# Regrouping the attention half of a transformer block, and three smaller moves: halves on GpSimd, gate tiles on SyncE's queue, block outputs in two pieces

## The chip, the cores and the metric

One Trainium2 chip, one core of it. A core has TensorE (PE: matmuls, with the weight load shown apart as PEld), VectorE (DVE), ScalarE (ACT), GpSimd (POOL) and SyncE (SP), which here only issues DMAs. ACT and POOL issue DMAs too; in the rows ACTq and SPq are the DMA issues of these engines. The metric is the device time of one execution in microseconds (us), median over runs.

## The reference

One layer on x of 1024 tokens by 1024 features, batch 1, all float32:

```
h  = rms_norm(x) ; y = h @ w_in              # q (8 heads of 64), k, v (2 heads), p (512)
a  = sliding-window attention(q, k, v)       # 64-token chunks, own and two before, q/k norm, bias, sinks
b  = pool_mixer(p)                           # trailing means over 2, 4, 8, 16 tokens, small matmuls
x  = x + concat(a, b) @ w_out
h2 = rms_norm(x)                             # "second norm"
q  = h2 @ wq ; top 16 of 128 keys, twice, for 8 heads ; top 16 of the 256 sums -> experts, gates
x  = x + sum over the 128 chosen experts of  gate * gelu(u[e] . h2) * v[e]
```

There are 128 x 128 = 16384 experts; u and v have one row of 1024 each per expert.

## The kernel before, in words

The 1024 tokens are 8 tiles of 128. Two ways of evaluating the experts stand side by side. Tiles 0, 6 and 7 are *gathered*: for each of 128 slots, GpSimd fetches one u row per token (L169), DVE takes the dot product (L190), and later the same with v rows (L197). Tiles 1 to 5 are *dense*: all experts in 128 blocks of 128, with matmuls. For a block, `load` (L227) fetches 512 KB of u into a `ur` buffer (there are three), `split` makes `uh` on ACT (L239) and the remainder `ul` on GpSimd (L244), and `u_mm` (L277) does 48 matmuls with 320 columns into two PSUM tiles, against `hh`/`hl`, the two halves of the transposed second norm of the dense tiles, which `halves` makes (L253 to L259). After gelu comes the product with the block's gates (L968), and then the v matmuls (L989).

The program has a front and a back. The front:

- `first(tiles)`: norm, projection by w_in, transposes. It is called for the sets in `FIRST`.
- `second(tiles)`: attention, pooling, the product with w_out (its weights streamed once per call, 16 DMAs of 256 KB, each split into `woh` on ACT, L357, and `wol` on DVE or GpSimd, L358, as `LOS2` says), second norm, and transposes to `h2Td` in DRAM (L668 to L670). It is called once for each entry of `GROUPS`; the tiles of one entry go through attention interleaved. `AT` says beside which group each later `first` set runs.
- `zero`: keys and top 16 for tile 0, so that its gathers can start early.
- `scores`: for the other seven tiles, 16 rounds of h2 @ wq and key scores (L782, L791), each followed on DVE by two top-8 searches per tile (`top16`, L674 to L679).
- for each tile `topk`, and for dense tiles `gates`: DVE builds one-hot tiles (L813, L820), PE multiplies them (L827), ACT evicts into `stage` (L829), and each of 20 full stage tiles of 2 MB goes out to `gd` (L833).
- `ahead`: 68 of the 128 u blocks are run in the front, as filler of the lowest priority; gelu results `wr` (L296) go to DRAM in `ad` (L297). `AHEAD0` of them are recorded beside the last group, before `scores`. The `ur` buffers are handed out in the order in which the code asks for them, and the halves of tiles 6 and 7, which `scores` needs, ask behind these blocks.

The back runs the other 60 u blocks, reads `gd` (L931) and `ad` (L953) back, and does all v matmuls; gathers run beside them.

A scheduler at build time orders the instructions of each engine; on the chip each engine runs its own list in that order, and a DMA that an engine issues waits for its inputs in the same list.

Of the kernel before, what the change touches and what calls it, by code (L numbers as in the profile page):

```python
# [8 lines left out]
F32 = mybir.dt.float32  # L9
# [5 lines left out]
AF = mybir.ActivationFunctionType  # L15
OP = mybir.AluOpType
AX = mybir.AxisListType

T, D, P = 1024, 1024, 128
# [8 lines left out]
LOW = -3.0e38  # L28


GROUPS = ((0,), (1, 2), (3, 4), (5, 6), (7,))
GSCALE = 32768.0
EARLY = 0.2
EARLY2 = 0.4
# [10 lines left out]
XB = 2  # L45
WPO = 2
WRB = 2
AHEAD0 = 8
HITP = 0
ULP = 4  # L50
VLP = 2
# [4 lines left out]
YQ = 3  # L56
WR0 = 4
SPLIT0 = 1
AT = (-1, 0, 2, 3)
GB0 = 2  # L60
WF = 3
QT = 3
# [6 lines left out]
WP = 3  # L69
XT = 1  # L70
LOS = (1, 1, 2, 2)
LOS2 = (1, 1, 1, 2, 1)
GAP = 0
AHP = 10000
VBUFS = 4
# [15 lines left out]
DT = ND * P  # L91
NH = DT // 2
# [3 lines left out]
TCH = 32  # L96
# [31 lines left out]
def body(tc, ctx, a):  # L128
    nc = tc.nc
# [4 lines left out]
    V, S, E, Q = nc.vector, nc.scalar, nc.tensor, nc.gpsimd  # L134
# [11 lines left out]
    gd = DR.tile([KEYS // CHUNK, P, NTC, CHUNK, TCH], F32, name="gd")  # L146
# [70 lines left out]
    U = {}  # L217
# [4 lines left out]
    ad = DR.tile([KEYS, P, DT], F32, name="ad")  # L222

    def load(b, h=None):
        if h is None:
            t = U["u"].tile([P, D], F32, name="ur", bufs=UR)
            nc.sync.dma_start(t, a["uT"][b].rearrange("p c e -> p (c e)"))  # L227
        else:
            t = U["v"].tile([P, 512], F32, name="vr", bufs=VR)
            nc.sync.dma_start(t, a["v"][b * KEYS:(b + 1) * KEYS, h * 512:(h + 1) * 512])  # L230
        raw[b, h] = t

    def split(b, h=None):
        t = raw.pop((b, h))
        if h is None:
            hi, lo = (U["u"].tile([P, D], F32R, name=n, bufs=2) for n in ("uh", "ul"))
        else:
            hi, lo = (U["v"].tile([P, 512], F32R, name=n, bufs=VBUFS) for n in (f"v{h}h", f"v{h}l"))
        S.activation(hi, t, AF.Copy)  # L239
        if h is None:  # L240

            for c in range(0, D, D // ULP):
                part = slice(c, c + D // ULP)
                Q.tensor_tensor(lo[:, part], t[:, part], hi[:, part], op=OP.subtract)  # L244
        elif h:
            for c in range(0, 512, 512 // VLP):
                part = slice(c, c + 512 // VLP)
                Q.tensor_tensor(lo[:, part], t[:, part], hi[:, part], op=OP.subtract)  # L248
        else:
            V.tensor_tensor(lo, t, hi, op=OP.subtract)  # L250
        us[b, h] = (hi, lo)

    def halves(i, hi, lo):  # L253
        t = U["u"].tile([P, D], F32, name="ur", bufs=UR)
        nc.sync.dma_start(t, h2Td[i])
        t3 = t.rearrange("p (c n) -> p c n", c=DC)
        S.activation(hi, t3, AF.Copy)
        V.tensor_tensor(lo, t3, hi, op=OP.subtract)
        return hi, lo  # L259

    def open_u():
# [7 lines left out]
    def u_mm(b):  # L269
        uh, ul = (t.rearrange("p (c e) -> p c e", c=DC) for t in us.pop((b, None)))  # L270
        pa = []
        after["turn"] = not after.get("turn")
        for n in range(2):
            p = PS.tile([P, 512], F32, name="pu", bufs=2) if b in soon or after["turn"] else ps()
            for k, (l, r) in enumerate(((uh, U["hh"]), (uh, U["hl"]), (ul, U["hh"]))):
                for d in range(DC):
                    E.matmul(p[:, :NH], l[:, d, :], r[:, d, n * NH:(n + 1) * NH],  # L277
                             start=(k == 0 and d == 0), stop=(k == 2 and d == DC - 1))
            pa.append(p)
        return pa  # L280

    def ahead():
        if AHEAD:
            with tc.high_priority(offset=-AHP):
                load(after[None])
                split(after[None])
        for b in soon:
            with tc.high_priority(offset=-AHP):
                if after[b] is not None:
                    load(after[b])  # L290
                pa = u_mm(b)
                if after[b] is not None:
                    split(after[b])
                t = U["u"].tile([P, DT], F32, name="wr", bufs=WRB)
                for n in range(2):
                    S.activation(t[:, n * NH:(n + 1) * NH], pa[n][:, :NH], AF.Gelu)  # L296
                nc.scalar.dma_start(ad[b], t)  # L297
            yield

    with ExitStack() as c1:  # L300
# [8 lines left out]
def front(tc, ctx, a, env):  # L309
    nc = tc.nc  # L310
    C, PS, DR, EX, ps, flow = (env[k] for k in ("C", "PS", "DR", "EX", "ps", "flow"))
    x1d, h2d, h2Td, gd = (env[k] for k in ("x1d", "h2d", "h2Td", "gd"))
    V, S, E, Q = nc.vector, nc.scalar, nc.tensor, nc.gpsimd
# [314 lines left out]
    def second(tiles):  # L628
        Y = {i: carry.pop(("first", i)) for i in tiles}
        wo = Stream(W, [a["w_out"][k] for k in range(8)], "wo", LOS2[GROUPS.index(tiles)], WPO, WRO, 1)  # L630
        if PAIR:
# [169 lines left out]
    def gates(i):  # L801
        j = DENSE.index(i)
        ekT, gT = carry["G", i]
        for q in range(P // TCH):
            sg = M.tile([P, KEYS, TCH], F32, name="stage", bufs=2)
            for r in range(TCH // TG):
                t0 = q * TCH + r * TG

                pairs = lambda x: x.rearrange("p (q w) -> p q w", w=2)[:, :, None, :].to_broadcast([P, TG // 2, P, 2])
                ob = []  # L810
                for s in range(2):
                    o = M.tile([P, TG // 2, P, 2], F16, name=f"ob{s}", bufs=OB)
                    V.tensor_tensor(o, pairs(ekT[:, s, t0:t0 + TG]),  # L813
                                    late["iote"][:, None, :, :].to_broadcast([P, TG // 2, P, 2]), op=OP.is_equal)
                    ob.append(o)
                    yield
                og = []
                for s in range(2):
                    o = M.tile([P, TG // 2, P, 2], F16, name=f"og{s}", bufs=OB)
                    V.tensor_tensor(o, ob[1], pairs(gT[:, s, t0:t0 + TG]), op=OP.mult)  # L820
                    og.append(o)
                    yield
                for h in range(TG // 4):
                    p = ps()
                    for t in range(4):
                        for s in range(2):
                            E.matmul(p[:, t * KEYS:(t + 1) * KEYS], ob[0][:, h * 2 + t // 2, :, t % 2], og[s][:, h * 2 + t // 2, :, t % 2],  # L827
                                     start=(s == 0), stop=(s == 1))
                    S.activation(sg[:, :, r * TG + h * 4:r * TG + h * 4 + 4], p.rearrange("p (t e) -> p e t", t=4),  # L829
                                 AF.Copy, scale=1.0 / GSCALE)  # L830
                    if h % 2:
                        yield
            nc.scalar.dma_start(gd[:, :, j * (P // TCH) + q].rearrange("c p e t -> p c (e t)"),  # L833
                              sg.rearrange("p (c e) t -> p c (e t)", e=CHUNK))
            yield

# [4 lines left out]
    def merge(parts, rate):  # L841
        parts = [[g, n, 0] for g, n in parts]
        total = max(n for _, n, _ in parts)
        for s in range(total):
            for part in parts:
                while part[2] * total < (s + 1) * part[1]:
                    part[2] += 1
                    next(part[0], None)
            flow(rate)
        for part in parts:  # L850
            for _ in part[0]:
                pass
# [4 lines left out]
    def lift(gen, by):  # L857
        while True:
            with tc.high_priority(offset=by):
                if next(gen, "end") == "end":  # L860
                    return
            yield
    merge([A1(FIRST[0])], 0)
    early1.close()
    W1 = early1.enter_context(tc.tile_pool(name="early1", bufs=2, reuse_waits="tile"))
    firsts = lambda k: [A1(f) for f, at in zip(FIRST, AT) if at == k]
    merge([A2(GROUPS[0])] + firsts(0), 0)
    X.open("tile0")
    M.tile = X.tile

    def zero():
        t = X.tile([P, DC, P], F32, name="h0T")
        nc.sync.dma_start(t, h2Td[0].rearrange("p (c t) -> p c t", c=DC))
        yield from scores((0,), [(t, None)], False)
        yield from topk(0)

    merge([A2(GROUPS[1]), (lift(zero(), HPZ), ZN)] + firsts(1), 0)
    X.close()
    open_g()
    for k in range(2, len(GROUPS) - 1):  # L880
        merge([A2(GROUPS[k])] + firsts(k), EARLY)
    early1.close()
    hh, hl = env["open_u"]()
    ahead = env["ahead"]()
    merge([A2(GROUPS[-1]), (islice(ahead, AHEAD0), AHEAD0)], EARLY)
    early.close()
# [11 lines left out]
    for i in ORDER:  # L898
# [3 lines left out]
        n = parts[0][1]  # L902
# [164 lines left out]
```

## Time and profile before

| | us |
|---|---|
| median of 3 runs (lowest, highest) | 2647.17 (2643.72, 2656.37) |
| profiled execution: time, span | 2642.85, 2641.1 |
| PE / DVE / POOL / ACT busy over the span | 2441.8 / 2244.3 / 1643.6 / 924.1 |

The span falls into stages, cut at events on PE: attention up to the first score matmul at 517.2; the score rounds up to 745.0; top-k and gates up to the last gate matmul at 1291.1; from there to the first v matmul at 1341.5; the back up to 2611.3; and a rest of gathers. Shares of busy time are means over stages with different limits, so they are read per stage. The profiled execution lies 4.3 us under the median of the runs.

### The profile page before, as it was taken

To read this page: it belongs to the slowest core of one execution; us is meant where nothing else is said; L and a number is where in the kernel's file an instruction comes from. 1 tells how busy PE (TensorE), PEld (TensorE's weight loads), DVE (VectorE), ACT (ScalarE), POOL (GpSimd) and SP (SyncE) were. 2 spreads that over 40 slices of the span, in tenths; PEclk is the share of its full clock that TensorE was granted. 3 is DMA by queue.
4 is the path that set the end of the run, shared out by engine and by line. 5 is a ranking of instruction groups with operands and counts; after the bars stand their busy time and mean duration, and the time that the engine had idled before them with its cause. 6 is when DMAs were issued, how large, how long until landed. Compare 5 with 4: busy or idle time off the path is not lost.

```text
span 2641.1 us, 41309 instructions
## 1 busy us (share of the span) xinstructions
PE 2441.8 (92%) x14627; PEld 2183.2 (83%) x14627; DVE 2244.3 (85%) x4236; ACT 924.1 (35%) x1701; POOL 1643.6 (62%) x1636
## 2 busy tenths in 40 slices
PE   7889776999998997989799999999999999999995
PEld 6678555999998887889798888888888888888884
DVE  4768776499999998999678888898898988889898
ACT  5646454322223444444342222322323222222221
POOL 1101765664566766666666767766777767667675
PEclk9989887999999998998899999999999999999998
DMA  7655779977677687777889999999999999999998
GB/s 238 224 172 174 263 244 314 340 241 246 213 261 256 202 270 255 218 230 252 299 286 353 356 332 348 342 329 347 340 348 336 346 348 346 326 354 335 335 332 313
DMA packets 323375, 770.22 MB, mean 292 GB/s; under 512 B 26944, under 2 KB 124128, under 8 KB 319072
## 3 DMA queue, kind: packets, MB, share of 16 engines
q0 software_dynamic: 110592, 402.70, 42.3%
q1 hardware_dynamic: 115072, 287.55, 31.9%
q10 hardware_dynamic: 97504, 77.34, 9.0%
q8 instruction: 114, 1.87, 0.3%
q14 instruction: 93, 0.76, 0.1%
HBM read 687.53 MB, written 79.95 MB: 291 GB/s over the span
## 4 chain that ended last, share of the span: by engine, by line
PE 47%; DVE 1%; issue 1%; DMA 1%; ACTq 0%; POOL 0%; ACT 0%; POOLq 0%; DVEq 0%
PE pt L989 16%; PE ps L989 16%; PE pu L277 8%; PE pt L277 4%; PE ps L277 4%; DVE vec L197 1%; DMA row<-v,idx 1%; ACTq L297 0%; POOL row L169 0%; DVE wl L977 0%; DVE wb L968 0%; DVE acc L994 0%; ACT wh L975 0%; ACT uh L239 0%; ACT row L200 0%
## 5 line engine op out<-in xcount | busy, mean ns | idle before, releaser
L244 POOL TENSOR_TENSOR ul<-ur,uh 128x256 fp32r<-128x256 f32 x512 | 462.3, 934 | 113.8 <-ACT uh L239 70.4
L169 POOL DMA_INDIRECT row<-v,idx x301 | 347.3, 1154 | 230.7 <-DVE vec L197 137.9
L169 POOL DMA_INDIRECT row<-u,idx x306 | 313.4, 1024 | 243.6 <-DVE row L190 118.8
L190 DVE SCALAR_TENSOR_TENSOR row<-row,vec 128x1024 f32<-128x1024 f32 x306 | 368.0, 1212 | 75.6 <-DMA row<-u,idx 72.2
L197 DVE SCALAR_TENSOR_TENSOR vec<-row,act,vec 128x1024 f32<-128x1024 f32 x301 | 385.6, 1281 | 25.4 <-DMA row<-v,idx 22.1
L277 PE MATMUL pu<-hh,uh 128*128 128x320 f32 x1568 | 283.3, 318 | 40.6 <-ACT wr L296 40.2
L277 PE MATMUL pu<-hh,ul 128*128 128x320 f32 x1568 | 281.7, 316 | 18.9 <-POOL ul L244 18.5
L277 PEld LDWEIGHTS pu<-hh,uh 128*128 128x128 f32 x1568 | 246.0, 193 | 54.1 <-ACT wr L296 48.9
L277 PE MATMUL pu<-hl,uh 128*128 128x320 f32 x1568 | 276.7, 314 | 0.0
L277 PEld LDWEIGHTS pu<-hh,ul 128*128 128x128 f32 x1568 | 246.0, 192 | 24.8 <-POOL ul L244 21.8
L277 PEld LDWEIGHTS pu<-hl,uh 128*128 128x128 f32 x1568 | 246.8, 192 | 2.7
L248 POOL TENSOR_TENSOR v1l<-vr,v1h 128x256 fp32r<-128x256 f32 x256 | 210.4, 848 | 11.8 <-ACT v1h L239 8.9
L239 ACT ACTIVATE uh<-ur 128x1024 fp32r<-128x1024 f32 x128 | 135.1, 1058 | 235.4 <-PE pu L277 126.3
L975 ACT ACTIVATE wh<-wb 128x640 fp32r<-128x640 f32 x128 | 91.6, 735 | 216.6 <-PE ps L989 123.0
L239 ACT ACTIVATE v0h<-vr 128x512 fp32r<-128x512 f32 x128 | 80.5, 631 | 241.2 <-DMA vr<-v 151.9
L989 PE MATMUL pt<-v0h,wh 128*128 128x512 f32 x384 | 150.6, 392 | 3.3 <-ACT wh L975 2.6
L989 PE MATMUL pt<-v0h,wl 128*128 128x512 f32 x384 | 150.6, 393 | 0.2 <-DVE wl L977 0.2
L989 PE MATMUL pt<-v0l,wh 128*128 128x512 f32 x384 | 149.7, 390 | 0.0
L989 PE MATMUL ps<-v1h,wh 128*128 128x512 f32 x384 | 149.4, 389 | 0.0
L989 PE MATMUL ps<-v1h,wl 128*128 128x512 f32 x384 | 149.4, 389 | 0.0
L989 PE MATMUL ps<-v1l,wh 128*128 128x512 f32 x384 | 149.4, 389 | 0.0
L994 DVE TENSOR_TENSOR acc<-pt,acc 128x512 f32<-128x512 f32 x155 | 106.2, 685 | 42.9 <-PE pt L989 42.5
(267 smaller groups left out, 5846.6 us busy)
## 6 DMA issues: line engine op xcount, KB each, us to landing
ur<-uT SPq DMA_DIRECT2D x128, 512.0 KB, 4.7
vr<-v SPq DMA_DIRECT2D x256, 256.0 KB, 6.1
gd<-stage ACTq DMA_DIRECT2D x20, 2048.0 KB, 12.3
g<-gd SPq DMA_DIRECT2D x32, 1280.0 KB, 8.5
ad<-wr ACTq DMA_DIRECT2D x68, 320.0 KB, 5.2
wb<-ad SPq DMA_DIRECT2D x68, 320.0 KB, 6.7
wo<-w_out SPq DMA_DIRECT2D x80, 256.0 KB, 4.2
wi<-w_in SPq DMA_DIRECT2D x32, 512.0 KB, 4.7
```

The lines of the kernel that those rows point to most:

```text
L169: Q.indirect_dma_start(out=r, out_offset=None, in_=tabs[s], in_offset=bass.IndirectOffsetOnAxis(ap=EX[i][0][:, k:k + 1], axis=0))
L190: V.scalar_tensor_tensor(r, r, 1.0, vec, op0=OP.mult, op1=OP.mult, accum_out=st["act"][:, k:k + 1])
L197: V.scalar_tensor_tensor(vec, r, st["gl"][:, k:k + 1], vec, op0=OP.mult, op1=OP.add)
L239: S.activation(hi, t, AF.Copy)
L244: Q.tensor_tensor(lo[:, part], t[:, part], hi[:, part], op=OP.subtract)
L248: Q.tensor_tensor(lo[:, part], t[:, part], hi[:, part], op=OP.subtract)
L277: E.matmul(p[:, :NH], l[:, d, :], r[:, d, n * NH:(n + 1) * NH], start=(k == 0 and d == 0), stop=(k == 2 and d == DC - 1))
L975: S.activation(wh, wr, AF.Copy)
L989: E.matmul(p, l[:, j * P:(j + 1) * P], r, start=(m == 0 and k == 0), stop=(m == CHUNK - 1 and k == 2))
L994: V.tensor_tensor(part, p, part, op=OP.add)
```

## The change

`GROUPS` has four pairs, so w_out is streamed four times; `LOS2` and `AT` follow (`first` of tiles 5, 6 now runs beside the group (2, 3) and tile 0's keys, `first` of tile 7 beside (4, 5)). `AHEAD0` goes from 8 to 12. The remainder in `halves` is taken by GpSimd. Each `wr` is two tiles of 320 columns, each sent by its own DMA. The gate tiles are sent by SyncE in place of ScalarE.

```diff
-GROUPS = ((0,), (1, 2), (3, 4), (5, 6), (7,))
+GROUPS = ((0, 1), (2, 3), (4, 5), (6, 7))
-AHEAD0 = 8
+AHEAD0 = 12
-AT = (-1, 0, 2, 3)
+AT = (-1, 0, 1, 2)
-LOS2 = (1, 1, 1, 2, 1)
+LOS2 = (1, 1, 2, 1)
@@ halves
-        V.tensor_tensor(lo, t3, hi, op=OP.subtract)
+        Q.tensor_tensor(lo, t3, hi, op=OP.subtract)
@@ ahead
-                t = U["u"].tile([P, DT], F32, name="wr", bufs=WRB)
                 for n in range(2):
-                    S.activation(t[:, n * NH:(n + 1) * NH], pa[n][:, :NH], AF.Gelu)
-                nc.scalar.dma_start(ad[b], t)
+                    t = U["u"].tile([P, NH], F32, name="wr", bufs=2 * WRB)
+                    S.activation(t, pa[n][:, :NH], AF.Gelu)
+                    nc.scalar.dma_start(ad[b, :, n * NH:(n + 1) * NH], t)
@@ gates
-            nc.scalar.dma_start(gd[:, :, j * (P // TCH) + q].rearrange("c p e t -> p c (e t)"),
+            nc.sync.dma_start(gd[:, :, j * (P // TCH) + q].rearrange("c p e t -> p c (e t)"),
```

PE's list at the first round of scores. In the names `uh`, `ul` are a u block's halves, `wqh`, `wql` those of wq, `gh`, `gl` those of the second norm of tiles 6 and 7, and `sk` the keys (L791 gives one tile's scores). Before:

```order
L782 MATMUL ps<-hh,wqh 128x320 x8
L782 MATMUL ps<-hl,wqh 128x320 x8
L782 MATMUL pt<-hh,wqh 128x320 x8
L782 MATMUL pt<-hl,wqh 128x320 x8
L782 MATMUL ps<-gh,wqh 128x256 x3
L782 MATMUL ps<-hh,wql 128x320 x8
L782 MATMUL pt<-hh,wql 128x320 x8
L782 MATMUL ps<-gh,wqh 128x256 x5
L782 MATMUL ps<-gl,wqh 128x256 x8
L782 MATMUL ps<-gh,wql 128x256 x8
L791 MATMUL pt<-sk,qT 128x128 x2
```

And now, from the last piece of the round's dense part:

```order
L277 MATMUL pu<-hl,uh 128x320 x5
L791 MATMUL pt<-sk,qT 128x128 x2
L277 MATMUL pu<-hl,uh 128x320 x3
L277 MATMUL pu<-hh,ul 128x320
L791 MATMUL pt<-sk,qT 128x128 x2
L782 MATMUL pt<-hh,wqh 128x320 x8
L782 MATMUL pt<-hl,wqh 128x320 x8
L782 MATMUL pt<-hh,wql 128x320 x8
L277 MATMUL pu<-hh,ul 128x320 x7
L277 MATMUL pu<-hh,uh 128x320 x8
L277 MATMUL pu<-hl,uh 128x320 x8
```

The round was one piece, with the `gh` matmuls of tiles 6 and 7 inside; now the `gh` part is not there: four tiles are scored, the next round's dense part goes first, and u blocks follow, 151 matmuls in a row. Counted over the whole list, 433 u matmuls stood before the round's last score and 586 do now (48 are a block); before the last L668 it was 311 and is 216.

SyncE's list in the gate stage (`ur<-uT` is the load of a u block, `gd<-stage` a gate tile). Before:

```order
L758 DMA wq<-wq 128x1024
L759 DMA sk<-skT 128x128
L181 DMA rowx<-x1d 128x1024
L227 DMA ur<-uT 128x1024 x55
L230 DMA vr<-v 128x512 x3
L931 DMA g<-gd 128x2560 x2
```

And now:

```order
L181 DMA rowx<-x1d 128x1024
L227 DMA ur<-uT 128x1024 x18
L833 DMA gd<-stage 128x32x128
L227 DMA ur<-uT 128x1024 x2
L833 DMA gd<-stage 128x32x128 x2
L227 DMA ur<-uT 128x1024 x2
L833 DMA gd<-stage 128x32x128
L227 DMA ur<-uT 128x1024 x4
L833 DMA gd<-stage 128x32x128
L227 DMA ur<-uT 128x1024
```

The 20 gate tiles stand between loads of u blocks, mostly one to five loads apart.

ScalarE's list at the last gate tile. Before:

```order
L829 ACTIVATE stage<-ps 128x128x4
L296 ACTIVATE wr<-pu 128x320 x2
L833 DMA gd<-stage 128x32x128
L297 DMA ad<-wr 128x640
L239 ACTIVATE uh<-ur 128x1024
L296 ACTIVATE wr<-pu 128x320
L297 DMA ad<-wr 128x640
```

And now:

```order
L297 DMA ad<-wr 128x320
L829 ACTIVATE stage<-pt 128x128x4
L297 DMA ad<-wr 128x320
L829 ACTIVATE stage<-ps 128x128x4
L961 ACTIVATE pu<-pu 128x320
L239 ACTIVATE uh<-ur 128x1024
L296 ACTIVATE wr<-pu 128x320
L297 DMA ad<-wr 128x320
```

No gate tile is issued between ACT's own work any more, and the first block of the back (L961) comes sooner: PE's list has 216 u matmuls between the last gate matmul and the first v matmul, and had 269.

## Rows read from the trace of the kernel before

**Rows 1.** Windows of the stages: length, busy us (xinstructions), clock, DMA share, GB/s.

```profile
core 0: us, PE busy (x) PEld busy (x) DVE busy (x) ACT busy (x) POOL busy (x), PEclk, DMA share, GB/s
0.00:517.20 517.20, 427.41 (x2404) 346.16 (x2405) 351.40 (x761) 270.26 (x624) 199.19 (x185) 0.92 0.73 243
517.20:745.00 227.80, 216.62 (x1573) 213.93 (x1572) 207.29 (x912) 59.60 (x110) 124.23 (x110) 0.99 0.72 242
745.00:1291.10 546.10, 486.50 (x3856) 468.44 (x3855) 522.28 (x1003) 229.38 (x378) 373.09 (x307) 0.95 0.75 244
1291.10:1341.50 50.40, 41.69 (x274) 41.16 (x272) 20.73 (x23) 14.61 (x25) 27.85 (x34) 0.93 0.91 326
1341.50:2611.30 1269.80, 1266.30 (x6516) 1111.17 (x6515) 1119.82 (x1521) 349.26 (x564) 907.92 (x988) 1.00 0.94 339
```

**Rows 2.** Chain that ended last, one u block: start us, us, what.

```profile
1327.54 7.04 PE pu L277 x48
```

**Rows 3.** Timeline of PE, first scores: start us, us, engine, line, op.

```profile
533.17 0.61 PE L791 MATMUL ps<-sk,qT 128*128 128x128 f32 x4
```

**Rows 4.** Windows of the attention stage, columns as in rows 1.

```profile
64.00:145.00 81.00, 62.68 (x343) 49.27 (x344) 60.91 (x129) 60.71 (x160) 14.00 (x12) 0.89 0.67 214
...
340.00:428.00 88.00, 62.63 (x310) 43.82 (x308) 63.72 (x103) 47.30 (x117) 55.70 (x47) 0.87 0.76 251
428.00:500.00 72.00, 65.26 (x381) 58.58 (x380) 43.29 (x67) 27.32 (x43) 44.51 (x52) 0.88 0.94 334
sum 436.00, PE 359.27 PEld 289.71 DVE 316.06 ACT 230.89 POOL 181.69; mean PE 71.85 PEld 57.94 DVE 63.21 ACT 46.18 POOL 36.34
```

**Rows 5.** Timeline of PE, two of its idles there, in brackets with the releaser.

```profile
76.39 1.94 PE L533 MATMUL ps<-ident,prob 128*128 128x128 f32 x8 [5.71 <-ACT xh L586]
...
423.82 2.93 PE L668 MATMUL pt<-ident,x 128*128 128x128 f32 x12 [8.61 <-DVE x L660]
```

**Rows 6.** Lines L258 and L773: ns min/median/max, first and last start.

```profile
L258 DVE TENSOR_TENSOR gl<-ur,gh x2: 1219/1220/1221, 509.4 to 519.4; 128x1024 fp32r<-128x1024 f32 x2
...
L773 POOL TENSOR_TENSOR wql<-wq,wqh x16: 2376/2406/2432, 521.4 to 714.1; 128x1024 fp32r<-128x1024 f32 x16
```

**Rows 7.** Waits of DVE, 745 to 1291.1: us in total, times, longest.

```profile
DVE vec L197 <- DMA rowx<-v,idx: 6.8, 5, 3.2
DVE gate L726 <- PE ps L743: 6.1, 1, 6.1
```

**Rows 8.** Waits of PE in the same stretch.

```profile
PE pu L277 <- ACT wr L296: 31.5, 22, 5.3
```

**Rows 9.** Timeline of ACT behind the last gate tile.

```profile
1292.14 1.85 ACTq L833 DMA_DIRECT2D gd<-stage  x1
...
1294.04 12.53 ACTq L297 DMA_DIRECT2D ad<-wr  x1
```

**Rows 10.** Timeline of PE there.

```profile
1308.12 2.50 PE L277 MATMUL pu<-hh,uh 128*128 128x320 f32 x8 [8.33 <-ACT wr L296]
```

**Rows 11.** DMA issues of the page: count, KB each, us from issue to landing.

```profile
ur<-uT SPq DMA_DIRECT2D x128, 512.0 KB, 4.7
...
gd<-stage ACTq DMA_DIRECT2D x20, 2048.0 KB, 12.3
```

**Rows 12.** Waits of the SP queue, 840 to 1300.

```profile
SPq L227 <- POOL ul L244: 313.6, 43, 17.4
SPq L227 <- ACT uh L239: 125.7, 28, 12.6
```

**Rows 13.** DMA issues, 1280 to 1345.

```profile
g<-gd SPq DMA_DIRECT2D x3, 1280.0 KB, 8.2
...
gd<-stage ACTq DMA_DIRECT2D x1, 2048.0 KB, 18.0
```

**Rows 14.** Timeline of DVE at the start of the back.

```profile
1324.24 0.88 DVE L968 TENSOR_TENSOR wb<-pu,g 128x320 f32<-128x320 f32 x2
```

**Rows 15.** Line L197 from 1341.5 on: ns min/median/max.

```profile
L197 DVE SCALAR_TENSOR_TENSOR vec<-row,act,vec x227: 1271/1280/1291, 1340.6 to 2633.4; 128x1024 f32<-128x1024 f32 x114
```

## The prediction

> **What bounds the kernel now.** I read the windows by stage first, since the page's shares mix stages with different limits. The back is PE's: 1266.3 us busy of 1269.8 [rows 1]. The change touches nothing that PE does there, so its length stays, and so does the rest of gathers behind it: both lists of DVE end in the same 13 gathers behind the last v product. The question is when the back starts. In the gate stage the reader is to see DVE at 522.3 of 546.1 us, with PE at 486.5: DVE is idle 24 us, PE 60, and the direct waits of DVE are short [rows 1, 7]. The score stage has both near full (PE 216.6 and DVE 207.3 of 227.8). In the attention stage nothing is full: PE 427.4 of 517.2, DVE 351.4. So work taken off DVE or PE in the attention stage only counts if it brings forward the moment from which DVE has the score rounds to do. I call this moment R: the end of the first round of scores, 533.8 (533.17 and 0.61) [rows 3]. From R to the last gate DVE is the limit, and from the last gate to the first v matmul PE and a chain of transfers. The time of the whole is R, plus the DVE stretch, plus this passage, plus what is fixed.
>
> **The change, part by part.**
>
> *R, the work in front of it.* The list of PE has 586 u matmuls in front of the end of the round, and had 433. A block of 48 takes 7.04 us at full clock [rows 2], so 153 more are 22.4 us; 27 more score matmuls of the next round, with as many columns or fewer, come to about 3 us at the 0.147 us that a u matmul has there. Together +25 us. It is not new work, only moved forward: PE has 3 blocks less later, but later DVE is the limit and PE has room, so there it gives nothing back. The cause is the order in which `ur` buffers are handed out: the halves of tiles 6 and 7 ask behind 12 blocks, not 8. Bounds: the count is exact; PE could fall behind or find the blocks in holes, which is the next term.
>
> *R, the idle time in front of it.* Five groups make five times the chain scores, maximum, exp, transposes, product, norm, and PE has 436 - 359.3 = 76.7 us without work between 64 and 500 [rows 4], with idles such as 5.71 us in the lone tile 0 and 8.61 us at the norm of tiles 5 and 6 [rows 5]. With four groups one such chain goes; a fifth of 76.7 is 15 us. The clock there is 0.88 to 0.89, and 0.92 over the stage [rows 1, 4], so of the 359 busy us some 30 to 40 are matmuls stretched by the lower of the two levels, which PE gets after idle stretches; a fifth is 7, and I count 3, since other idles remain. Sum -18. Lower bound 0: two pairs could take as long as two lone tiles and a pair. Upper bound 28: the idle time of the two lone stretches, 81 - 62.7 = 18 and 72 - 65.3 = 7 [rows 4], and 3. In between I take the mean chain because the pairs that remain also had less filler than before: the keys of tile 0 now run beside `first` of tiles 5 and 6. One stream of w_out less (16 loads, 16 splits on ACT, 16 on DVE) is part of this; neither engine is full in the stage.
>
> *Halves on GpSimd.* Seven instructions of 1.22 us leave DVE; on GpSimd a remainder of that shape takes 2.41 us [rows 6]. POOL is busy 199 of 517 us [rows 1], and in front of the `gh` matmuls stand 151 u matmuls, 22 us. Cost 0; if this cover were gone, 2 times 1.2 us.
>
> *Blocks in two pieces.* 68 more issues on ACT, which is busy 229 of 546 us in the gate stage [rows 1]; the first piece leaves earlier. I cost it at 0: what hides it is ACT's own idle time. Bounded by -3 and +3 us (a few of the waits of PE for `wr` [rows 8]).
>
> *Gate tiles on SyncE's queue.* Behind a gate tile the next issue on ACT's queue is held: 12.53 us at the last one, and PE is idle 8.33 us for it [rows 9, 10]. In the gate stage PE waits 31.5 us for ACT's `wr` [rows 8]. This goes, but DVE, not PE, is the limit there, so at most DVE's 24 idle us can come back; DVE's waits for PE (6.1 us and smaller ones) are of this kind, its waits for gathers are not [rows 7]. I take -8, a third of it. On SP the tile is now in front of loads of u blocks: 12.3 us for a tile and 4.7 for a load make 17 us [rows 11] for a load that is caught behind one. SP does almost nothing but wait for free buffers, 439 of 460 us [rows 12], so a load goes out two blocks ahead; the list has 53.4 blocks in the 546 us of the gate stage, 10.2 us each, and 20 us of room. Cost 0. If the room is 2 us short for all 20 tiles, PE is 40 us late in sum, of which DVE would feel 24 in 60, as now: bounds -24 and +16.
>
> The Trainium skill (DMA: Bandwidth & Descriptors, "Issuing engines are not separate DMA queues") says that DMAs from different engines run on the same 16 DMA engines, and that another issuer saves only the issue time, usually small. Here the issue itself took 12.53 us [rows 9], so the trace shows a price of the issuer that is not small. By the rule alone this term would be 0; that is the second rival.
>
> *The passage into the back.* It took 1341.5 - 1291.1 = 50.4 us [rows 1]. PE has 216 u matmuls in it and had 269: 31.7 us in place of 39.5; and the 8.33 us go. But the first v matmuls need the gates: the last tile was issued 1 us behind the last gate matmul and landed 18.0 us later, `g` took 8.2 [rows 9, 13], which is 27; then DVE has three `v0l` and, for four blocks, eight products (0.88 us for two [rows 14]) and four remainders, some 10 us. That is 37, later than PE's 31.7: here is the new wait, some 5 us of PE. So 50.4 becomes 37, -13. Bounds -19 (31.7, transfers faster) and -3 (the tile lands 10 us later on SP's queue).
>
> *Gathers.* Six v gathers fewer lie in front of the back (122, were 128). They cost DVE 6 times 1.28 us [rows 15] in the back, where it is busy 1119.8 of 1269.8 us [rows 1]: hidden, 7.7 us if not.
>
> Sum: 25 - 18 - 8 - 13 = -14. The profiled execution took 2642.85 us (its span of 2641.1 and 1.75 around it), so 2628.9; the median of the runs stands 4.3 us over it, so the forecast is 2633.
>
> **The rivals.**
>
> *Scores late (slower).* If the pairs keep the idle time of the five chains (-5 in place of -18), R moves by +20, the whole DVE stretch with it, and with nothing back in the gate stage and the short end of the passage (-3): 25 - 5 - 3 = +17, 2664. For it speaks that DVE is full from R on [rows 1]; against it the idles of the lone groups [rows 4, 5]. It decides from R later than about 548.
>
> *The queue only moves the wait.* SP's loads come late by what ACT gains, the gate stage gains nothing and loses 4, and the last tile is as late as before (-5): 25 - 18 + 4 - 5 = +6, 2653. For it: one ring now carries gate tiles and u loads, 17 us against some 20 of room. Against it: SP's long waits for buffers.
>
> *Both come out well (faster).* All of the lone idle time goes (-27), DVE gets most of its 24 us (-20), the passage -16: -38, 2609. For it: idle lowers the clock, so the two add up. Against it: DVE waits more for gathers than for ACT or PE.
>
> **How the numbers follow.** Forecast 0.45, scores late 0.17, the queue 0.18, both well 0.20. About 0.5%, 13 us, is what a measurement of this kernel can tell from no change: faster is under 2634, slower over 2660. The forecast, with its own range of 2622 to 2646, lies on that edge: 0.25 faster, 0.20 same. Both well is faster, 0.20. The queue: 0.15 same, 0.03 slower. Scores late: 0.12 slower, 0.05 same. Sums 0.45, 0.40, 0.15. For 8 in 10 the range reaches to the centre of the fast case and nearly to that of the slow one: 2609 to 2659.
>
> **What would show it.** R at 533.8 + 7 = 541, with 12 blocks done in front of it. No issue over 5 us on ACT's queue. Wide rooms between a u load and its `uh` on ACT; waits of ACT's `uh` for the load would show the second rival. In the gate stage DVE over 0.96. Behind the last gate PE waits for `wh` or `wl` before its first v matmul. The prediction is wrong if R comes earlier than 525 or later than 550, or if the time moves while R, the gate stage and the passage together don't.

## The result, and the profile after

The changed kernel takes 2677.69 us (median of 7 runs, 2674.25 to 2683.99), the kernel before, run beside it, 2647.17 (7 runs, 2643.72 to 2661.56): ratio 1.0098, interval 1.0078 to 1.0118. It is slower by 1%; the forecast was 2633, with a range up to 2659. In the profiled executions the spans are 2676.5 and 2641.1, 35.4 us apart; that is 5 us more than the medians are, since the profiled execution of the kernel before lies 4.3 us under its median and that of the changed kernel 1.3 over it. One execution of a run further down, e7, took 10732.67 us, four times the others, and its median and ratio are given without it.

The windows of the changed kernel, cut at the events of [rows 1] (first matmul of the late stage, end of the scores, last gate, first v matmul, end of the last v matmul, end); columns as there:

```profile
0.00:512.10 512.10, 418.43 (x2332) 335.45 (x2333) 310.08 (x705) 260.20 (x602) 190.67 (x169) 0.93 0.66 218
512.10:778.50 266.40, 253.29 (x1811) 249.03 (x1810) 220.65 (x939) 69.20 (x126) 154.16 (x145) 0.99 0.76 249
778.50:1306.20 527.70, 466.18 (x3745) 445.57 (x3744) 519.62 (x1002) 224.20 (x373) 351.31 (x294) 0.97 0.78 247
1306.20:1349.30 43.10, 33.76 (x216) 32.97 (x216) 20.40 (x23) 11.63 (x20) 23.72 (x30) 0.88 0.98 353
1349.30:2641.90 1292.60, 1276.40 (x6530) 1113.33 (x6528) 1127.17 (x1524) 348.07 (x565) 904.64 (x991) 1.00 0.92 333
2641.90:2676.50 34.60, 0.00 (x0) 0.00 (x0) 27.68 (x22) 1.02 (x1) 14.84 (x16) 0.54 0.83 332
```

The last two of these stretches in the kernel before. [rows 1] end its back at 2611.3; its last v matmul ends at 2614.6, and from here on the back is taken up to there:

```profile
1341.50:2614.60 1273.10, 1269.57 (x6529) 1113.55 (x6527) 1122.69 (x1523) 349.26 (x564) 909.97 (x991) 1.00 0.94 339
2614.60:2641.10 26.50, 0.00 (x0) 0.00 (x0) 19.94 (x16) 1.02 (x1) 9.28 (x10) 0.58 0.77 309
```

Read as differences: the first v matmul is 7.8 us later (1349.3, was 1341.5), the back is 19.5 longer (1292.6, was 1273.1), and the end behind it 8.1 longer (34.6, was 26.5). The forecast had -14 for the first and nothing for the other two, where 27.6 of the 35.4 us lie. Within the front, R is at 566.4 (was 533.8 in [rows 3]), so it has moved by 32.6 and not by 7:

```profile
565.77 0.61 PE L791 MATMUL ps<-sk,qT 128*128 128x128 f32 x4
```

The way from R to the last gate takes 739.8 us, was 757.5, and DVE is busy 519.62 of 527.70 in the gate stage, which is nearly all. The passage takes 43.1, was 50.1.

### The profile page after: what moved, and what is told of

The parts are those of the page before. It is cut to its first block, busy times and chain, and to the rows that moved or that the text cites. A ratio compares the mean times of both kernels' runs of the same rounds, so it can differ in the third digit from the quotient of the medians.

```text
span 2676.5 us, 41337 instructions
## 1 busy us (share of the span) xinstructions
PE 2448.1 (91%) x14627; PEld 2176.4 (81%) x14627; DVE 2225.6 (83%) x4213; ACT 914.3 (34%) x1685; POOL 1639.3 (61%) x1643
## 5 line engine op out<-in xcount | busy, mean ns | idle before, releaser
L169 POOL DMA_INDIRECT row<-v,idx x302 | 330.5, 1094 | 259.0 <-DVE vec L197 138.3
L169 POOL DMA_INDIRECT row<-u,idx x304 | 298.6, 982 | 261.8 <-DVE row L190 128.7
L197 DVE SCALAR_TENSOR_TENSOR vec<-row,act,vec 128x1024 f32<-128x1024 f32 x302 | 387.5, 1283 | 39.1 <-DMA row<-v,idx 35.5
L248 POOL TENSOR_TENSOR v1l<-vr,v1h 128x256 fp32r<-128x256 f32 x256 | 209.1, 842 | 13.6 <-ACT v1h L239 11.8
L977 DVE TENSOR_TENSOR wl<-wb,wh 128x640 fp32r<-128x640 f32 x128 | 138.7, 1098 | 16.8 <-ACT wh L975 14.5
L169 POOL DMA_INDIRECT rowx<-v,idx x82 | 102.8, 1253 | 81.2 <-DVE vec L197 34.9
```

The source lines that it names most:

```text
L169: Q.indirect_dma_start(out=r, out_offset=None, in_=tabs[s], in_offset=bass.IndirectOffsetOnAxis(ap=EX[i][0][:, k:k + 1], axis=0))
L197: V.scalar_tensor_tensor(vec, r, st["gl"][:, k:k + 1], vec, op0=OP.mult, op1=OP.add)
L977: V.tensor_tensor(wl, wr, wh, op=OP.subtract)
```

## The experiments

Each run is the kernel before (B) or the changed one (A) with some parts swapped. Parts: g the groups (with `AT`, `LOS2`), a `AHEAD0 = 12`, h the remainder of the halves on GpSimd, w blocks in pieces, q gate tiles on SyncE's queue. Event times are those of each profiled execution, in us: the last h2T transpose, R, the last gate, the first v matmul, the length of the back, the end behind it. "Products" are the gather products of DVE (768 in all) that have started by R and by the first v matmul; "behind" those behind the last v matmul. "PE waits" are the waits of PE in the back.

| run | parts | median | ratio | h2T | R | gate | first v | back | end | products | behind | PE waits |
|---|---|---|---|---|---|---|---|---|---|---|---|---|
| before | B | 2647.2 | 1 | 499.6 | 533.8 | 1291.3 | 1341.5 | 1273.1 | 26.5 | 66, 239 | 15 | 3.5 |
| after | B+gahwq | 2677.7 | 1.0098 | 489.1 | 566.4 | 1306.2 | 1349.3 | 1292.6 | 34.6 | 61, 232 | 21 | 16.3 |
| e1 | B+g | 2672.6 | 1.0086 | 481.6 | 526.0 | 1303.3 | 1350.4 | 1280.6 | 43.6 | 51, 226 | 28 | 6.7 |
| e2 | A-g | 2683.9 | 1.0127 | 523.5 | 589.2 | 1350.6 | 1389.1 | 1295.6 | 13.2 | 78, 249 | 5 | 16.1 |
| e3 | A-a | 2671.2 | 1.0087 | 492.6 | 535.7 | 1274.9 | 1351.2 | 1284.7 | 29.5 | 49, 232 | 16 | 10.7 |
| e4 | B+q | 2637.6 | 0.9964 | 499.1 | 533.0 | 1283.1 | 1333.3 | 1279.1 | 22.7 | 66, 240 | 12 | 8.1 |
| e5 | A-h | 2653.8 | 1.0020 | 480.7 | 553.3 | 1296.0 | 1337.0 | 1283.9 | 35.1 | 61, 233 | 22 | 10.3 |
| e6 | B+h | 2659.6 | 1.0035 | 514.5 | 551.3 | 1305.3 | 1351.3 | 1292.6 | 19.3 | 69, 245 | 9 | 16.5 |
| e7 | B+qa | 2650.1 | 1.0008 | 501.1 | 554.2 | 1302.9 | 1339.1 | 1291.8 | 17.1 | 70, 243 | 8 | 15.0 |
| e8 | B+qw | 2651.1 | 1.0011 | 494.6 | 527.6 | 1271.9 | 1333.6 | 1298.6 | 14.7 | 64, 243 | 7 | 20.1 |
| e9 | A, no rows | 2626.6 | 0.9899 | 492.1 | 570.4 | 1319.5 | 1356.2 | 1269.3 | 3.7 | 61, 233 | 0 | 1.3 |
| e10 | B, no rows | 2622.0 | 0.9892 | 497.9 | 532.0 | 1296.6 | 1348.7 | 1267.8 | 3.9 | 66, 240 | 0 | 0.8 |
| e11 | A, half products | 2659.0 | 1.0018 | 489.4 | 567.5 | 1312.9 | 1353.0 | 1275.1 | 28.4 | 61, 232 | 18 | 5.4 |
| e12 | B+q again | 2638.2 | 0.9956 | 499.0 | 532.7 | 1278.6 | 1330.6 | 1280.8 | 23.5 | 66, 240 | 11 | 10.0 |

Each ratio is to B as it ran beside that run (medians 2647.2 to 2649.6). Intervals are within 0.0020 to 0.0027 of the ratio for e1 to e8, e11 and e12; some 0.006 for e9 (3 executions) and 0.0044 for e10 (2). Event times come from one execution each. All but one lie within 5.3 us of their median; that of e2 (2701.8) is the longest of its five and 18 us over it, so its event times stand too late. e4 and e12 are the same kernel: their events differ by up to 4.5 us and their backs by 1.7, which is a scale for how far two single profiles can be told apart.

**The groups alone (e1).** Theory: fewer gathers find room beside four groups, and those left stand in the back.

```
-GROUPS = ((0,), (1, 2), (3, 4), (5, 6), (7,))      AT = (-1, 0, 2, 3)   LOS2 = (1, 1, 1, 2, 1)
+GROUPS = ((0, 1), (2, 3), (4, 5), (6, 7))          AT = (-1, 0, 1, 2)   LOS2 = (1, 1, 2, 1)
```

> The kernel before with the four groups alone; AHEAD0 stays 8, gate tiles stay on ACT's queue, blocks whole, halves on DVE. In the order of the program 9.0 u blocks stand in front of the end of the first score round, as before, and 28 v gathers stand behind the last v product (before 15, the whole change 21); 243 gathers are done when the first v product is taken up (before 256). Theory 'gathers' (the four pairs leave fewer gathers beside the attention, and those left over stand in the back and behind its end): the end behind the last v matmul grows from 26.5 us by 13 x 1.32 = 17 us to about 44, the back by 10 to 25 us, sum 2670 to 2690. Rival 'blocks in front of the scores' (the 12 blocks of AHEAD0 make everything behind them late): nothing of this is here, R comes at 534 or up to 18 us earlier, 2630 to 2650.

Measured: slower by 0.9%, inside the first theory's range, with the end as it said and the back only 7.5 us longer, where 10 to 25 were expected. The last transposes come 18.0 us earlier, but R only 7.8, and 51 products have started by then in place of 66. What is lost between transposes and R is u blocks: fewer of them found room in the shorter attention, so 165 u matmuls (27.4 us of PE) start between the last transposes and R, where the kernel before has 122 (18.2 us). By the first v matmul 13 products are still missing and the lead is gone (+8.9); the end is 17.1 us longer. What the groups saved in front was time in which PE did u blocks and DVE did gathers.

**All but the groups (e2).** A with `GROUPS`, `AT`, `LOS2` of before (the diff above, reversed).

> The changed kernel with the five groups of before: AHEAD0 is 12, gate tiles on SyncE's queue, blocks in halves, halves' remainder on GpSimd. In the order 12.2 u blocks stand in front of the end of the first score round, as in the changed kernel; 263 gathers are done when the first v product is taken up and 5 v gathers stand behind the last one (changed kernel 250 and 21). Theory 'gathers': the end behind the last v matmul falls to about 26.5 - 13 = 14 us, the back to its 1273 us or less, the gate stage keeps the gain of the whole change, so 2605 to 2635 in spite of a late R. Rival 'blocks in front of the scores': R at 555 to 570 and the time as late as with the whole change, 2660 to 2680.

Measured: 2683.9, above both theories. The end shrinks to 13.2 as the first theory has it, but the back does not shrink with it, and the attention itself is late: transposes at 523.5, R at 589.2 in place of 555 to 570. So the groups are not the whole cause, and something among a, h, w, q slows the attention. Taking the groups out of A does not make it faster (1.0127, with them 1.0098), though alone they cost 0.9%: the parts do not add.

**`AHEAD0` back at 8 (e3).**

```
-AHEAD0 = 12
+AHEAD0 = 8
```

> The changed kernel with AHEAD0 back at 8. In the order 8.2 u blocks stand in front of the end of the first score round (12.2 in the changed kernel), 251 gathers are done at the first v product (250), and 16 v gathers stand behind the last one (21). Theory 'blocks in front of the scores': R goes back by 4 blocks x 7.04 = 28 us to about 538, and the time with it, 2640 to 2655. Theory 'gathers': R goes back too, but the gathers left over are the same within one, so the back stays at about 1293 us and the gate stage gives up most of the gain, only the end gets shorter by 5 x 1.32 = 7 us: 2660 to 2675.

Measured: 2671.2, in the second theory's range. R goes back by 30.7, as both said, and the last gate by 31.3, but the passage grows to 76.3 us with 436 u matmuls in it (A: 43.1 with 216), so the first v matmul stays. The back is 1284.7 and not 1293, which neither theory has. Its row, beside the fourth of the windows of A:

```profile
1274.90:1351.20 76.30, 67.51 (x436) 66.20 (x435) 31.05 (x32) 24.70 (x41) 50.19 (x61) 0.93 0.90 323
```

The blocks in front of R are not lost: here, what they cost there comes back in the passage.

**Gate tiles alone (e4, and e12, the same kernel once more).**

```
-            nc.scalar.dma_start(gd[:, :, j * (P // TCH) + q]...
+            nc.sync.dma_start(gd[:, :, j * (P // TCH) + q]...
```

> The kernel before with nothing but the gate tiles issued by SyncE in place of ACT. The order in front of the gates is that of before; 11 v gathers stand behind the last v product (before 15). If the queue was the cause of the 26 us that the gate stage lost in length from before to after, it goes from 393 to about 370 us here too, no ACT issue over 5 us is left, and with 4 gathers less at the end (5 us) the time is 2615 to 2625. If the gate stage got shorter only because it started late and work in it had been done ahead (4 gathers fewer stand in it, and its u blocks), it stays at 385 to 393 us and the time at 2635 to 2645.

> The kernel of the fourth run once more, gate tiles on SyncE's queue alone, in more rounds: there it took 0.9964 [0.9944, 0.9984] of the time before. If its gate stage is shorter in every execution, as in the profile (384 against 393 us), the ratio stays between 0.994 and 0.998 and the profile shows the first v product at 1330 to 1336 again (before 1341.5); if it was one lucky profile, the ratio is 0.999 or more.

Measured: 0.9964 and 0.9956, so this part is a gain of some 10 us, and its kernel is the fastest complete one here. The time of 2615 to 2625 that the first theory of e4 had is missed by far; 2637.6 lies in the range of the second. The gain itself came again in e12, as expected there. From R to the last gate it takes 750.1 and 745.9 us, before 757.5 (first before, then e4, then e12; columns as in [rows 1]):

```profile
533.80:1291.30 757.50, 688.16 (x5319) 667.62 (x5319) 720.78 (x1887) 283.21 (x479) 483.63 (x407) 0.96 0.74 240
```

```profile
533.00:1283.10 750.10, 684.16 (x5321) 661.85 (x5321) 718.92 (x1886) 284.17 (x479) 483.87 (x407) 0.97 0.75 244
```

```profile
532.70:1278.60 745.90, 682.27 (x5322) 661.62 (x5322) 718.87 (x1885) 284.21 (x478) 483.09 (x407) 0.97 0.75 244
```

DVE's idle time there falls from 36.7 to 31.2 and 27.0 us, which is most of the gain. In the kernel before, ACT waited 22.8 us for pieces of the way to `ad`, and eight issues on its queue took 3 to 12.5 us; the first row is a wait of ACT before, 745 to 1291.1 (total, times, longest):

```profile
ACT wr L296 <- DMA ad<-wr: 22.8, 5, 8.7
```

In e4 and in A that wait is gone (A has 2.4 us of the kind, at `uh`), the longest such issue in the gate stage is 2.0 us in A and 1.2 in e4, and ACT's `uh` waits for no load in either.

**Halves back on DVE (e5) and halves alone (e6).**

```
-        Q.tensor_tensor(lo, t3, hi, op=OP.subtract)
+        V.tensor_tensor(lo, t3, hi, op=OP.subtract)
```

> The changed kernel with the remainder of the halves back on DVE. Theory 'POOL's list' (seven remainders of 2.4 us stand in the list of GpSimd in front of splits of w_out, factors of norms and gather issues, and hold them in the attention): the stretch from the h2T transposes of tiles 2 and 3 to those of 4 and 5, 164 us in the changed kernel against 152 with the groups alone, falls to 150 to 156, the last transposes end at 475 to 482 in place of 489, R at 550 to 558 in place of 566, and the time is 8 to 15 us shorter, 2660 to 2670. Rival 'the pieces of wr or AHEAD0 hold it': all of this stays within 3 us, and the time at 2675 to 2685, a little longer for the 1.2 us remainders on DVE.

> The kernel before with the remainder of the halves on GpSimd and nothing else. Theory 'POOL's list': between the transposes of tile 4 and of tiles 5 and 6 the program needs 10 us more than its 85, as the run without the groups did (99), the last transposes end at 508 to 520 in place of 499.6 and the first v product comes 8 to 20 us later; 9 v gathers in place of 15 stand behind the last v product, which gives 8 us back: 2648 to 2665. Rival: the cover of 22 us of u matmuls in front of gh holds, 2636 to 2648.

Measured: by the ratios, e5 takes some 21 us less than A, more than the theory said, and e6 some 10 more than B, as it said. In e5 the transposes come 8.4 earlier, R 13.1, the first v matmul 12.3, and the back is 8.7 shorter, which the theory did not have; in e6 the events come 14.9, 17.5 and 9.8 later than before. The list of POOL in A, where tiles 4 and 5 run (start, us, engine, line, operation, idle before):

```profile
344.54 0.94 POOL L169 DMA_INDIRECT row<-u,idx  x1 [3.25 <-DVE row L190]
345.50 2.39 POOL L258 TENSOR_TENSOR hl<-ur,hh 128x1024 fp32r<-128x1024 f32 x1
347.85 1.27 POOL L358 TENSOR_TENSOR wol<-wo,woh 128x512 fp32r<-128x512 f32 x1
349.08 2.38 POOL L258 TENSOR_TENSOR hl<-ur,hh 128x1024 fp32r<-128x1024 f32 x1
351.43 1.27 POOL L358 TENSOR_TENSOR wol<-wo,woh 128x512 fp32r<-128x512 f32 x1
352.68 2.37 POOL L258 TENSOR_TENSOR hl<-ur,hh 128x1024 fp32r<-128x1024 f32 x1
355.20 0.95 POOL L169 DMA_INDIRECT row<-u,idx  x1 [0.16 <-issue]
```

For 10 us POOL has almost no idle time, and splits of w_out and row issues stand behind remainders. Over this stretch (249 to 413 in A, 247.6 to 402.4 in e5) PE waits 6.3 us for POOL's `wol` (e5: 1.0) and DVE 20.2 for rows (13.6). The longest stop of PE in it comes by way of DVE, which stands before a late row; behind that row in its list is the norm (`x`, L660) that PE's transposes need (DVE, then PE):

```profile
405.66 1.22 DVE L190 SCALAR_TENSOR_TENSOR row<-row,vec 128x1024 f32<-128x1024 f32 x1 [5.31 <-DMA row<-u,idx]
408.21 1.97 PE L668 MATMUL pt<-ident,x 128*128 128x128 f32 x8 [9.99 <-DVE x L660]
```

That this row is late because of the remainders on POOL is not shown. The stretch between tile 4 and tiles 5 and 6, first before and then in e6:

```profile
340.60:428.40 87.80, 62.40 (x307) 43.22 (x306) 63.52 (x104) 46.70 (x115) 55.28 (x47) 0.87 0.77 252
```

```profile
341.60:440.30 98.70, 67.16 (x307) 48.23 (x306) 61.56 (x107) 46.77 (x115) 67.20 (x55) 0.79 0.73 242
```

POOL has 12 us more to do and the stretch is 11 longer; PE takes 4.8 us more for the same 307 matmuls, with the clock at 0.79 in place of 0.87. This part makes up 14.9 of the 23.9 us by which e2's transposes are late; the rest is not told apart.

**Queue and `AHEAD0` (e7), queue and pieces (e8).**

```
e7 -AHEAD0 = 8
   +AHEAD0 = 12
e8 -                t = U["u"].tile([P, DT], F32, name="wr", bufs=WRB)
   +                    t = U["u"].tile([P, NH], F32, name="wr", bufs=2 * WRB)
```

> The kernel before with gate tiles on SyncE's queue and AHEAD0 at 12; five groups, halves on DVE, whole blocks. 11.3 u blocks stand in front of the end of the first score round (before 9.0), 69.0 in front of the last gate (66.4), and 8 v gathers behind the last v product (15). Theory 'blocks moved are given back': R is 16 us later (550), the last gate 10 to 15 us later, the passage shorter by 2.6 blocks, 18 us, so that the first v product comes within 8 us of the 1333 of the queue alone, and the time is 2630 to 2645. The prediction's own step, that blocks moved forward give nothing back later: first v product at 1349, time 2650 or more.

> The kernel before with gate tiles on SyncE's queue and blocks sent in halves. If the pieces are free (the prediction took 0, between -3 and +3), the transposes end at 499 as with the queue alone; 260 gathers are done at the first v product (with the queue alone 256) and 7 v gathers stand behind the last one (11): 2630 to 2638. If the pieces are what made the run without the groups late in the attention, the last transposes end at 510 or later and the time is over 2645.

Measured: the first v matmul comes at 1339.1 (5.8 later than in e4, R 21 later) and 1333.6 (the same), and the end shrinks, much as the theories said. Yet the times are out of the ranges that go with this (2630 to 2645, 2630 to 2638): both are some 12 us over e4's (1.0008 and 1.0011, e4 0.9964), and the back is 1291.8 and 1298.6 long, 13 and 20 us more than in e4. Neither edit touches the back, and at the first v matmul 3 products fewer are left to do.

**No rows (e9, e10), half products (e11).** What lengthens the back? In e9 and e10 the row fetches of the back go, in e11 half of each product (the code is shown shortened). These three runs leave out part of the output.

```
e9, e10 +  if st.get("more"):                  # in the back
        +      rows[st["issued"]] = st["fix"][0]; st["issued"] += 1; continue
e11     +  w = 512 if st.get("more") else D    # r[:, :w], vec[:, :w] in both products
```

> The changed kernel without the row transfers of the gathers in the back: from there on DVE multiplies one fixed row, as often and as wide as before, and no rows are fetched (the three gathered tiles of the output are left out of the computation). All 21 v gathers that stood behind the last v product now stand in front of it. Theory 'rows late' (DVE stands in its list before a row that hasn't landed, and PE's accumulators and wl behind it are late): the back falls from 1292.6 to 1268 to 1278 us although DVE has 21 products more in it, and PE's waits there from 16 to under 5 us. Rival 'DVE's own work' (the products of the gathers stand in front of acc, wb and wl whether their rows have landed or not): the back stays at 1285 to 1310.

> The kernel before with the same left out: no row transfers in the back, DVE multiplies a fixed row there, 384 times each as before (the three gathered tiles of the output are left out of the computation). The control for the run above. Theory 'rows late': 1266 to 1274 us, equal to the changed kernel without rows within 4 us, since nothing is left that differs in the back. Rival 'DVE's own work': 1280 to 1300 with 15 more products in it, and other than the changed kernel by 10 us or more.

> The changed kernel with the products of the gathers in the back on the first 512 of 1024 columns; every row is still fetched whole (half of each product is left out of the computation in the back). 18 v gathers stand behind the last v product (changed kernel 21). DVE's work in the back falls by some 490 x 0.6 = 290 us. Theory 'rows late': DVE still waits 20 us or more for rows there, and the back is at 1280 us or more. Rival 'DVE's own work': PE's waits fall under 5 us and the back to 1268 to 1276.

Measured, first the back of e9, then of e10, then of e11, columns as in [rows 1]:

```profile
1356.20:2625.50 1269.30, 1268.01 (x6530) 1113.98 (x6528) 1122.80 (x1544) 348.94 (x566) 403.05 (x481) 1.00 0.39 132
```

```profile
1348.70:2616.40 1267.70, 1266.93 (x6529) 1114.40 (x6528) 1115.78 (x1537) 349.08 (x565) 399.26 (x481) 1.00 0.39 132
```

```profile
1353.00:2628.10 1275.10, 1269.69 (x6530) 1113.67 (x6528) 873.91 (x1527) 348.64 (x565) 907.16 (x994) 1.00 0.93 340
```

Without rows both kernels have the same back within 1.6 us, although DVE works as much as before (1123 and 1116 us). The medians are 4.6 us apart in place of 30.5, but from 3 and 2 executions, and those of e9 spread over 17 us. With the rows but half the products, DVE is busy 873.91 us in place of 1127.17 and A's back is 1275.1, though DVE still waits 38 us for rows. So neither alone does it: rows that land late hurt where DVE, busy for 0.87 of the back, has little room to catch up. "Rows late" held for e9 and e10; in e11 its range for the back failed, and the rival was right on the back (1268 to 1276) and just missed on PE's waits (5.4, not under 5). Two things are not told apart. Without rows the DMA share falls from 0.92 to 0.39 and POOL's work from 904.64 to 403.05 us, so e9 also takes away whatever the rows do to other loads and to POOL's splits. And with other products in the back, the lists of e9 and e10 are ordered anew, as in every run.

## Why the prediction was wrong

**The back (the step that failed most).** "The back is PE's", and so its length stays: this did not hold, and the back is 19.5 us longer. PE is nearly full there only as long as DVE keeps up: its products wait for accumulators that DVE frees and for weights that DVE makes, and in DVE's list gather products stand between these. PE's waits in the back, first before and then after (total, times, longest):

```profile
PE pt L989 <- ACT wh L975: 2.6, 2, 1.9
PE pt L989 <- DVE acc L994: 0.7, 1, 0.7
PE pt L989 <- DVE wl L977: 0.2, 1, 0.2
```

```profile
PE pt L989 <- DVE acc L994: 4.0, 4, 1.8
PE pt L989 <- issue: 2.9, 2, 2.0
PE pt L989 <- DVE wl L977: 2.8, 5, 0.7
PE pt L989 <- ACT wh L975: 2.7, 2, 2.5
PE ps L989 <- DVE wb L968: 2.5, 3, 1.2
PE ps L989 <- DVE acc L994: 0.8, 1, 0.8
PE pu L277 <- DVE row L190: 0.6, 1, 0.6
```

3.5 us became 16.3, and 10.7 of these end with an instruction of DVE. The other 6.8 of the 19.5 us is PE's busy time (1276.40, was 1269.57). One stop in A; the list of DVE (idle time in brackets), then PE:

```profile
1478.61 1.55 DVE L977 TENSOR_TENSOR wl<-wb,wh 128x640 fp32r<-128x640 f32 x2
1485.82 1.22 DVE L190 SCALAR_TENSOR_TENSOR rowx<-rowx,vec 128x1024 f32<-128x1024 f32 x1 [5.66 <-DMA rowx<-u,idx]
1486.97 0.08 DVE L190 DVE_READ_ACCUMULATOR rowx<-rowx,vec 128x1 f32 x1
1486.97 0.69 DVE L994 TENSOR_TENSOR acc<-pt,acc 128x512 f32<-128x512 f32 x1
1487.71 0.51 PE L989 MATMUL pt<-v0h,wh 128*128 128x512 f32 x1 [1.81 <-DVE acc L994]
```

DVE stands 5.66 us before a row; the `acc` behind it was ready, and PE stops for 1.81. That late rows stand behind the other stops too is not shown one by one. The waits of DVE for rows in the back, first before and then after:

```profile
DVE row L190 <- DMA row<-u,idx: 13.9, 10, 3.6
...
DVE vec L197 <- DMA row<-v,idx: 9.3, 9, 2.1
...
DVE vec L197 <- DMA rowx<-v,idx: 4.3, 3, 3.5
...
DVE rowx L190 <- DMA rowx<-u,idx: 0.8, 1, 0.8
```

```profile
DVE vec L197 <- DMA row<-v,idx: 23.1, 13, 5.0
...
DVE rowx L190 <- DMA rowx<-u,idx: 8.5, 3, 5.7
DVE vec L197 <- DMA rowx<-v,idx: 7.4, 4, 3.1
...
DVE row L190 <- DMA row<-u,idx: 3.6, 2, 3.3
```

In sum 28.3 became 42.6. But this sum is not what orders the backs: e1 has 42.3 us of such waits, with PE waits of 6.7 and a back of 1280.6, and e5 has 17.9, with 10.3 and 1283.9. It matters which work of PE stands behind a late row, not how much is late. With PE's waits the length does go: over the eleven runs that compute everything, backs with 3.5 to 8.1 us of them are 1273 to 1281 long, with 10.0 to 10.7 1281 to 1285, and with 15 and more 1292 to 1299. Every edit lengthened the back, those that do not touch it too (e7, e8). In each, the list of DVE in the back is in another order: of its 514 gather products before, 325 (e7) to 378 (e8) keep their place among DVE's other work in a run that computes everything, even where the lists are shifted to match best. Why the order of before has so few stops of PE is not settled, and its back is known from one execution, which lies 4.3 us under the median. It isn't the number of products: 514 start in its back, 515 in A's, 518 in e8's.

**"Gathers: hidden, 7.7 us if not", and the 13 at the end of both lists.** The two lists were misread. 15 stand behind the last v matmul before and 21 after, 1.3 us each, and this end is 8.1 us longer: the 6 gathers that were missing in front were not hidden.

**R, the blocks, +25.** Their size at R is right: in e3 193 u matmuls fewer stand in front of R, which at the 0.147 us of the prediction is 28.3, and 30.7 were measured. But "there it gives nothing back" is not right: the passage is PE's, and the blocks done earlier are missing in it. The prediction had 53 of them in its term of the passage and did not set them against this one. At the first v matmul the blocks cost -1.9 (A against e3) and +5.8 (e7 against e4), not 25.

**R, the idle time, -18.** The transposes did come 18.0 us earlier with the groups alone. At R 7.8 were left, and the first v matmul came 8.9 us later than before. The time without work on PE was not free: with it went room for u blocks, of which 43 matmuls more now stand between the last transposes and R, and for DVE's gathers, of which 15 fewer had started by R. From R on DVE is nearly full, and 15 x 1.3 = 20 us is what these take. At R as a whole, 30.7 for the blocks, -7.8 for the groups, 13.1 for the halves, -5.4 for the pieces (e8 against e4) and -0.8 for the queue make 29.8, and 32.6 were measured in place of 7.

**Halves, 0.** Mis-sized: 12.3 us at the first v matmul (e5), 9.8 (e6), some 21 and 10 in the whole. The price was looked for in front of `gh`; it lay in the attention, where POOL's list is full for a while.

**Blocks in two pieces, 0.** At the first v matmul this is right: 1333.6 beside 1333.3 (e8, e4). But the time is some 12 us longer, all of it in the back, which the term did not look at.

**Gate tiles, -8.** Right in size and place: 7.4 and 11.6 us between R and the last gate, 5.5 and 9.7 of them DVE's idle time, and 8.2 and 10.9 at the first v matmul (e4, e12). The Trainium skill (DMA: Bandwidth & Descriptors, "Issuing engines are not separate DMA queues") has another issuer save the time to issue alone, usually small beside the DMA itself. The trace agrees that issue time is what goes, with a longest issue on ACT of 12.53 us before [rows 9] and 1.2 in e4; it does not agree that this is always small: 12.53 us stands beside the 18.0 in which the gate tile in front of it landed [rows 13], and the move was worth 0.4%.

**The passage, -13.** It was -7.0, and the new wait is there, 8.91 us in place of some 5, on `wb`: PE stops for DVE's products before the last u block.

```profile
1340.71 2.50 PE L277 MATMUL pu<-hh,uh 128*128 128x320 f32 x8 [8.91 <-DVE wb L968]
```

Of the rivals "scores late" came nearest: it set R later than 548 as its point, and R is at 566.4. Half of its mechanism is there. The stretch from R to the last gate moves with R when only the blocks change (739.2 us in e3 and 739.8 in A, 750.1 in e4 and 748.7 in e7). But the gate stage did gain and the passage gave blocks back, so the first v matmul is only 7.8 us late, and most of the loss lies behind it, where no rival looked.

## What to carry to other kernels

A full engine in a profile can be full because a second one just keeps up: before the length of its stage is called fixed, take from the trace how often it waits for that engine and what stands in front in the list there. Idle time on one engine is only a gain if the others did no work in it that will be missing later; count that work at the same event in both orders. Test the parts of a change alone: here only the queue was a gain by itself (0.9956), and the sum hid it. Don't add what the parts cost, either: the groups cost 0.9% alone, but A without them is no faster.

## Not expected of the hardware

Short stops of PE in the back can cost more than their own length. In A, after stops of 1.21, 0.42 and 2.48 us between 2000 and 2009, the granted clock has a mean of 0.70 over 5 us, between its levels of 1.2 and 2.4 GHz, and is back at the higher one behind it (columns as in [rows 1]):

```profile
2000.00:2005.00 5.00, 3.37 (x13) 2.02 (x12) 5.00 (x5) 2.30 (x4) 4.72 (x6) 1.00 0.82 297
2005.00:2010.00 5.00, 2.52 (x10) 1.53 (x9) 4.96 (x6) 0.74 (x1) 4.67 (x5) 0.95 0.95 338
2010.00:2015.00 5.00, 5.00 (x21) 4.28 (x21) 5.00 (x7) 0.74 (x1) 4.67 (x6) 0.70 0.75 254
2015.00:2020.00 5.00, 5.00 (x29) 4.50 (x28) 3.48 (x4) 0.42 (x1) 3.78 (x5) 1.00 0.92 352
```

By these rows (0.30 of 5 us and 0.05 of 5 us) this costs some 1.7 us, and it is the only such place in A's back. PE is busy 1276.40 us there, 1269.57 in the back before and 1266.93 in that of e10, with the same number of weight loads within one: 7 to 9.5 us more in the matmuls themselves, beside the waits. The clock explains some 1.7 of these; the rest stays open.

At the very end rows land about as fast as DVE multiplies whole ones. With half products (e11, 0.75 us) most products still start some 1.28 us apart, each behind a wait for its row, with PE idle and a DMA share of 0.87 (2634 to 2652):

```profile
2639.15 0.76 DVE L199 SCALAR_TENSOR_TENSOR vec<-row,act,vec 128x512 f32<-128x512 f32 x1 [0.52 <-DMA row<-v,idx]
2640.44 0.75 DVE L199 SCALAR_TENSOR_TENSOR vec<-row,act,vec 128x512 f32<-128x512 f32 x1 [0.54 <-DMA row<-v,idx]
```

So where the products are halved, the end goes on at the pace of the rows.
